# A hybrid decoder block on one core: down's weight sums built beside up instead of at the start, and a ninth pair of up by seven products

## The chip, the core and the metric

The kernel runs on one core of a Trainium2 chip. The metric is the device time of one execution in microseconds (us), and the kernel before is given by the median of three runs. The engines are named as the profile names them: PE (TensorE) multiplies matrices, DVE (VectorE) and ACT (ScalarE) do elementwise work, POOL (GpSimd) does a little elementwise work and issues some of the DMAs, SP (SyncE) issues the others. Each engine takes its own list of instructions strictly in order, and an instruction that has to wait holds up everything behind it on its engine.

## The reference

One layer of a decoder block on a sequence of 512 positions of width 1024, all in float32. The parts that matter here:

```python
mod = c_act @ ada_w[l] + ada_b[l]
shift1, scale1, gate1, shift2, scale2, gate2 = ...          # split of mod
h = rms_norm(x, norm1_g[l]) * (1 + scale1) + shift1
z = h @ w_in[l]
q, k, v, p, g_attn, g_pool = jnp.split(z, split_at, axis=-1)
...                                                         # attention of 8 heads, pooling, gates, merge
x = x + gate1 * (merged @ w_out[l])

h2 = rms_norm(x, norm2_g[l]) * (1 + scale2) + shift2
u = causal_dwconv(h2 @ w_up[l], conv_w[l], conv_b[l])       # w_up: 1024 x 5632
u_g, u_v = jnp.split(u, 2, axis=-1)
x = x + gate2 * ((jax.nn.silu(u_g) * u_v) @ w_down[l])      # w_down: 2816 x 1024
```

`ada_w` (1024 x 6144) is 25 MB, `w_up` 23 MB, `w_down` 11.5 MB.

## The kernel before

**Precision.** Every float32 operand of a product is split into a high part (`hi`, made by ACT) and the rest (`lo`, made by DVE), and a product is three matmuls, hi by hi, hi by lo and lo by hi (`mm3` and `more`, L131 to L141). A weight unit of 128 x 1024 (512 KB) is loaded by SP into one of five `wraw` buffers (`load_unit`, L82). SP's next load waits until DVE has read a buffer for the last time.

**The stages.** (1) Start: x is loaded, normalised and turned; then `p` and `q` are projected over eight channel blocks k. For each k, two units of `ada_w` (shift1 and scale1) must be loaded and summed by DVE (`sum_one`, L207) before h can be made, and for every two k there is a unit of p and one of q. (2) `k` and `v` projections. POOL takes a power of -0.5 for their norms (`hr_q`, `hr_k`, L520), DVE applies it (`n_q`, `n_k`, L528). (3) Eight heads of attention, filled up with the gate projections. (4) Branches and the output projection. (5) Up: 22 pairs j of a gate unit and a value unit. (6) Down: a Strassen-like form with seven products instead of eight, over 11 channel blocks, in seven phases.

**The weight sums.** Down's seven products need four sums of blocks of `w_down`, `t1 = b11+b12`, `t3 = b12+b22`, `t2 = t1+b22` and `t4 = b21+t2`, for eleven channel tiles kk. Ten of the tiles are made by DMAs alone (`t_step`): in six steps, a plain load fills two 256 KB buffers `ta` and `tc` (L794 is the load, L789 an accumulating DMA that adds a block of `w_down` to the buffer), and stores (L790) bring the results to HBM as `tsum`. All of these are on POOL's queue, eleven DMAs a tile, each of which waits for the one before it on its buffer. Four buffers (pool `wsum`) hold two tiles at a time. Down then loads the sums with SP (`raw_t`). Tile 4 is made by DVE instead: `t_get(4)` loads four blocks, `t_do(4)` adds them (L773 to L776), `t_put(4)` stores them.

In the code tiles 0 to 3 stand beside the heads (`t_steps(2 * h, ...)`) and tiles 5 to 10 beside the pairs of up. Only PE, DVE and ACT are issued in the order of the code (`manual_schedule`); POOL and SP are ordered by a scheduler, which puts an instruction as early as it believes that it can run. So the DMAs of tiles 0 to 3 stand at the very head of POOL's list, among the small operations of stages 1 and 2.

**Up.** A plain pair is two products of 8 blocks with 512 columns (48 matmuls). A pair in `SEVEN` (5, 7, ..., 19) is done by seven products with 256 columns (84 matmuls, `seven`), for which DVE and ACT prepare sums of the weights (`prep_seven`: steps s0 to s3, `ut`, `lo_upG`, `lo_upR`, `lo_upV`) one pair ahead; it also needs sums of h2 (`h_forms(n)`, n = 0 to 3, each two sums `hs`, two `hi` parts on ACT and two `lo` parts). Pairs 0 and 1 are multiplied ahead of the loop over j (`first`), in halves of 256 columns. At j their banks already hold the results, so the loop's first matmuls are those of pair 2. `behind(0)` is the convolution of the pair before (four DVE operations, L985 and L986) and `behind(1)` its gate (`glu_b`, two DVE operations).

**Down.** During phase 0 DVE and ACT split the weights `b11`, make the last two blocks' forms (`s_forms`) and split `s2`, which is used in phase 2.

Of the kernel before, what the change touches and what calls it, by code (L numbers as in the profile page):

```python
# [32 lines left out]
NU = (NP // 2 + 1) // 2  # L33

PLAIN = 3
SEVEN = (5, 7, 9, 11, 13, 15, 17, 19)
FORMS = ("b11", "t1", "t2", "b21", "t3", "b22", "t4")
ET = mybir.EngineType
ENG = {ET.PE, ET.DVE, ET.Activation}
# [16 lines left out]
def block_kernel(tc, x, cvec, ada, wtok, wch, pool_w, wbr, wout, wup, wdn, pack, table, out):  # L56
    nc = tc.nc
# [3 lines left out]
    with ctx:  # L61
# [692 lines left out]
        def t_tile(name):  # L754
            return tp_.tile([P, 512], F32, tag="t", name=name)

        def t_load(kk):
            i, u = divmod(kk, 2)
            b = {}
            for nm in ("b11", "b12", "b22", "b21"):  # L760
                b[nm] = t_tile(f"{nm}_{kk}")
                nc.gpsimd.dma_start(b[nm], wdn[plain[nm], i][:, u * 512 : u * 512 + 512])
            return b

        tb = {}

        def t_get(kk):
            tb[kk] = t_load(kk)

        def t_do(kk):  # L770

# [44 lines left out]
        gg = gate_stream()  # L816
        fill(gg, FIRST)
        share = (NG * 5.2 - FIRST) / H
        def t_steps(n, start, kks):

            for x_, kk in enumerate(kks):
                if 0 <= n - start - 3 * x_ < 6:
                    t_step(kk, n - start - 3 * x_)

        for h in range(H):
            pt = flip(h, rows)
            if h + 1 < H:
                rows = softmax(h + 1, *logits(h + 1))
            if h + 2 < H:
                bias_rows(h + 2)  # L830
            t_steps(2 * h, 0, range(4))
            fill(gg, 3)
            if h % 2 == 0 and h < 6:
                stacks(h // 2 + 1, False)
            elif h in (1, 3):
                stacks((h + 3) // 2, True)
            values(h, *pt)
            ada_col(2, h)
            if h == 5:
                pooling(3)  # L840
            if h == 6:
                pool_proj(3)

            t_steps(2 * h + 1, 0, range(4))
            fill(gg, 3 if h < 5 else (share - 3) / 2)
            if h < 5:
                ada_col(3, h)
            fill(gg, (share - 3) / 2)
# [89 lines left out]
        def out_norm(t):  # L938
            row = [xr[t, 0], xr[t, 1]]
            rs = rms_rows(row, f"y{t}")  # L940
            for f in range(2):
                n_ = slot(f"xn2_{t}_{f}")
                nc.vector.tensor_scalar(n_, row[f], rs, None, op0=ALU.mult)
                xn2[t, f] = n_
                x2d[t, f] = dpool.tile([P, 512], F32, name=f"x2d_{t}_{f}")
                nc.gpsimd.dma_start(x2d[t, f], row[f])

        for t in range(TT):
            for f in range(2):
                if (t, f) == (0, 0):  # L950
                    for t_ in range(2):
                        for f_ in range(2):
                            out_mm(t_, f_, 0, KT - 2)
                if (t, f) != (3, 0):
                    out_mm(t, f, KT - 2 if t < 2 else 0, KT)
                    out_post(t, f, ops[t, f])
                if late:
                    ada_col(4, late.pop(0))
                    if not late:
                        nc.vector.scalar_tensor_tensor(acol[:, 32:40], acol[:, 32:40], 1.0, pk[:, C_N2 : C_N2 + 8],  # L960
                                                       op0=ALU.add, op1=ALU.mult)
            out_norm(t)
            if t == 2:
                out_mm(3, 0, 0, KT)
                out_post(3, 0, ops[3, 0])
                flip_h2(1)
                t_get(4)

# [226 lines left out]
        for j in range(NP):  # L1197
            if j + 1 == NP:
                steps = [lambda: ahead("b11_0", 0), lambda: ahead("b11_0", 1)]
            else:  # L1200
                steps = [] if j < PLAIN else (prep_seven if j + 1 in SEVEN else prep_two)(j + 1)
            if j < 2:
                u = first[2 * j][1], first[2 * j + 1][1]
                if j == 0:
                    t_do(4)
                    t_put(4, nc.gpsimd)
                behind(0)
                if j == 1:
                    for st in prep_two(PLAIN):
                        st()  # L1210
                behind(1)
                h_forms(j)
            elif j in SEVEN:
                mine = [steps[0], lambda: behind(0), lambda: behind(1), steps[1]]
                u = seven(j, lambda n: mine[n]())
            else:
                if j < PLAIN:
                    for e in range(2):
                        upw[j, e] = ready.pop(f"up{2 * j + e}")
                u = [bank(f"u_{2 * j + e}") for e in range(2)]  # L1220
                for st in steps[:-1]:
                    st()
                up_mm(u[0], upw.pop((j, 0)), 0, S)
                behind(0)
                for st in steps[-1:]:
                    st()
                up_mm(u[1], upw.pop((j, 1)), 0, S)
                behind(1)
                if j in (2, 3):
                    h_forms(j)  # L1230
            pend.append((j, *u))
            t_steps(j, 1, range(5, 11))
            if j in ADA_AT:
                ada_col(5, ADA_AT[j])
        behind(0)
# [30 lines left out]
        def fetch(m, f):  # L1266
            for p in range(2):
                t = 2 * m + p
                x2[t, f] = slot(f"x2r_{t}_{f}")
                nc.gpsimd.dma_start(x2[t, f], x2d[t, f])  # L1270


# [4 lines left out]
        def step(acc, p, u, a, w, c0, c1, stop):  # L1277
            ac = slice(u * 256 + p * P, u * 256 + p * P + P)
            cs = slice(u * 512 + c0, u * 512 + c1)
            more(accs[acc][p][:, c0:c1], a[0][:, ac], a[1][:, ac], w[0][:, cs], w[1][:, cs],  # L1280
                 (acc, p) not in fresh, stop)
            fresh.add((acc, p))

        for n, (an, bn, acc) in enumerate(phases):
            last = n == len(phases) - 1
            held_ = []
            for i in range(NU):
                if n == 0 and i == 0:
                    ahead("b11_0", 3)
                w = unit(f"{bn}_{i}")  # L1290
                a = forms.pop((an, i))
                if last and i >= NU - 2:
                    held_.append((a, w, width(i) // 512))
                else:
                    for u in range(width(i) // 512):
                        for p in range(2):
                            step(acc, p, u, a, w, 0, 512, i == NU - 1 and u == width(i) // 512 - 1)
                if n == 0:
                    if i == 0:
                        s_forms(NU - 2)  # L1300
                    if i == 2:
                        s_forms(NU - 1)
                    split_s = fa["s2", i]
                    forms["s2", i] = split_act(split_s, f"s2_{i}", width(i) // 2)
                elif n == 1:
                    forms["a12", i] = split_act(fa["a12", i], f"a12_{i}", width(i) // 2)
                elif n == 2:
                    split_a("s3", i)
                    s2 = fa.pop(("s2", i))
                    nc.vector.tensor_add(s2, s2, fa.pop(("a12", i)))  # L1310
                    fa["s4", i] = s2
                elif n == 3:
                    split_a("s4", i)
                    split_a("a22", i)
            if last:
                for p in range(2):
                    for x_, (a, w, nu) in enumerate(held_):
                        for u in range(nu):
                            step(acc, p, u, a, w, 0, 512, x_ == len(held_) - 1 and u == nu - 1)
                    finish(p, 1, 0, "X")  # L1320
            if n == 0:
                keep("s1", "X")
            elif n == 1:
                keep("s5", "Y")
            elif n == 2:
                keep("s2", "X")
                fetch(0, 0)
            elif n == 3:
                for p in range(2):
                    finish(p, 0, 0, "Z", plus="s1")  # L1330
                fetch(1, 1)
            elif n == 4:
                for p in range(2):
                    finish(p, 1, 1, "X", minus=("s5", None))
                fetch(0, 1)
            elif n == 5:
                for p in range(2):
                    finish(p, 0, 1, "Y", minus=(None, "s2"))
                fetch(1, 0)
# [69 lines left out]
```

## Time and profile before

| | us |
|---|---|
| runs of the kernel before | 697.74, 703.54, 702.74 (median 702.74) |
| the profiled execution: its own time | 699.71 |
| the profiled execution: span from first to last instruction | 697.9 |
| PE busy in the span | 668.3 (96%) |
| DVE, ACT, POOL busy | 545.7, 367.1, 151.5 |
| matmuls | 3403 |
| moved by DMA | 139.37 MB, mean 200 GB/s |

A row of the timeline is: start and duration in us, engine, line, operation, what is written and read, how many were merged (x4), and in brackets how long the engine sat idle before it and what ended the wait. A row of the table by stretches is: from:to, length, then busy us of PE, of its weight loads, of DVE, ACT and POOL with counts, the granted clock of PE, the busy share of the DMA engines and GB/s. Matmuls overlap, so PE's rate is read from the distance between starts.

### The profile page before, as it was taken

Reading aid. Unit: us, or ns where it says so; the run is one execution under the profiler, and the core shown is the slowest. Engines: PE = TensorE matmul, PEld = TensorE weight load, DVE = VectorE, ACT = ScalarE, POOL = GpSimd, SP = SyncE. Lnnn points to the kernel's source line nnn. Section 1 sums busy time; section 2 is a strip of 40 time slices with the busy share of each in tenths; the row PEclk is TensorE's granted clock in tenths of the full one; section 3 lists DMA queues with packets and bytes.
Section 4 is the critical chain, followed back from the end, with each engine's and each line's share of the span. In section 5 each row is a group of like instructions: output and inputs, shape, how many; then the busy total and the mean of one; then the engine's idle time right before and its main releaser. Section 6 shows DMA issues by size and latency. Waiting matters only on the chain.

```text
span 697.9 us, 9445 instructions
## 1 busy us (share of the span) xinstructions
PE 668.3 (96%) x3403; PEld 567.0 (81%) x3403; DVE 545.7 (78%) x914; ACT 367.1 (53%) x631; POOL 151.5 (22%) x199
## 2 busy tenths in 40 slices
PE   7787898899999999999999999999999999999997
PEld 5565676788888888788899898889998888788886
DVE  5645697588887868887758999999898996978774
ACT  6423624466756446560364565565565563867440
POOL 5324073400000004561303434442000000001000
PEclk9989999899999999999999999999999999999999
DMA  8999769344445245769336999998334352566751
GB/s 316 336 344 338 235 170 292 113 135 136 137 162 184 96 147 122 260 216 336 142 102 199 226 289 246 309 251 245 107 121 151 76 180 81 183 229 230 291 194 60
DMA packets 44100, 139.37 MB, mean 200 GB/s; under 512 B 5795, under 2 KB 5964, under 8 KB 44054
## 3 DMA queue, kind: packets, MB, share of 16 engines
q1 hardware_dynamic: 28358, 98.23, 41.5%
q0 software_dynamic: 15696, 40.54, 22.2%
q8 instruction: 26, 0.43, 0.3%
q14 instruction: 20, 0.16, 0.1%
HBM read 123.00 MB, written 15.76 MB: 199 GB/s over the span
## 4 chain that ended last, share of the span: by engine, by line
PE 73%; DVE 5%; ACT 2%; issue 1%; POOL 0%; DMA 0%; DVEq 0%
PE u L133 7%; PE u L134 7%; PE u L135 7%; PE gate_ps L135 4%; PE gate_ps L134 4%; PE gate_ps L133 4%; PE X L141 2%; PE X L140 2%; PE X L139 2%; PE uX L141 2%; PE uX L139 2%; PE uX L140 2%; PE o L135 2%; PE o L133 2%; PE o L134 2%; PE Y L140 1%
## 5 line engine op out<-in xcount | busy, mean ns | idle before, releaser
L133 PE MATMUL u<-h2h,hi_up 128*128 128x512 f32 (+1 forms) x256 | 93.0, 363 | 0.0
L134 PE MATMUL u<-h2l,hi_up 128*128 128x512 f32 (+1 forms) x256 | 92.9, 363 | 0.0
L135 PE MATMUL u<-h2h,lo_up 128*128 128x512 f32 (+1 forms) x256 | 92.8, 362 | 0.0
L207 DVE CUSTOM_DVE_ANT_0 raw_ada<-raw_ada,cbc,pk 128x1024 f32<-128x1024 f32 x48 | 62.2, 1302 | 11.3 <-DMA raw_ada<-in_ada 9.5
L135 PEld LDWEIGHTS u<-h2h,lo_up 128*128 128x128 f32 x256 | 48.3, 189 | 7.6
L133 PEld LDWEIGHTS u<-h2h,hi_up 128*128 128x128 f32 x256 | 48.4, 189 | 7.3
L134 PEld LDWEIGHTS u<-h2l,hi_up 128*128 128x128 f32 x256 | 48.4, 189 | 7.2
L133 PE MATMUL gate_ps<-h_h,hi_gate 128*128 128x512 f32 x128 | 50.0, 390 | 0.0
L135 PE MATMUL gate_ps<-h_h,lo_gate 128*128 128x512 f32 x128 | 50.0, 390 | 0.0
L134 PE MATMUL gate_ps<-h_l,hi_gate 128*128 128x512 f32 x128 | 49.9, 390 | 0.0
L789 POOL DMA_DIRECT2D tc<-in_wdn x30 | 27.8, 928 | 26.6 <-DMA tc<-in_wdn 22.2
L124 DVE TENSOR_TENSOR lo_t<-raw_t,hi_t 128x1024 fp32r<-128x1024 f32 (+1 forms) x24 | 26.7, 1132 | 8.0 <-ACT hi_t L114 7.9
L114 ACT ACTIVATE hi_t<-raw_t 128x1024 fp32r<-128x1024 f32 (+1 forms) x24 | 23.7, 987 | 17.5 <-PE Y L141 8.4
L114 ACT ACTIVATE hi_up<-raw_up 128x1024 fp32r<-128x1024 f32 x28 | 29.2, 1050 | 4.3 <-PE u L134 4.3
L220 POOL TENSOR_TENSOR wo_l<-raw_wo,wo_h 128x512 fp32r<-128x512 f32 x16 | 25.6, 1620 | 20.3 <-ACT wo_h L219 16.5
L1083 DVE TENSOR_TENSOR lo_up<-raw_up,hi_up 128x1024 fp32r<-128x1024 f32 x22 | 26.7, 1220 | 2.9 <-ACT hi_up L114 2.9
L135 PEld LDWEIGHTS gate_ps<-h_h,lo_gate 128*128 128x128 f32 x128 | 24.0, 188 | 5.1
L133 PEld LDWEIGHTS gate_ps<-h_h,hi_gate 128*128 128x128 f32 x128 | 24.0, 188 | 4.6
L134 PEld LDWEIGHTS gate_ps<-h_l,hi_gate 128*128 128x128 f32 x128 | 24.0, 188 | 4.5
L605 ACT ACTIVATE L<-L,mn 128x512 f32<-128x512 f32 (+3 forms) x32 | 17.6, 552 | 19.2 <-DVE mn L601 19.2
L133 PE MATMUL o<-wo_h,mg_h 128*128 128x512 f32 x64 | 25.0, 391 | 0.0
L135 PE MATMUL o<-wo_h,mg_l 128*128 128x512 f32 x64 | 24.9, 389 | 0.0
(365 smaller groups left out, 2009.5 us busy)
## 6 DMA issues: line engine op xcount, KB each, us to landing
raw_ada<-in_ada SPq DMA_DIRECT2D x48, 512.0 KB, 5.4
raw_up<-in_wup SPq DMA_DIRECT2D x44, 512.0 KB, 5.5
tc<-in_wdn POOLq DMA_DIRECT2D x40, 256.0 KB, 6.6
raw_t<-tsum_t SPq DMA_DIRECT2D x20, 512.0 KB, 4.5
raw_gate<-in_wch SPq DMA_DIRECT2D x16, 512.0 KB, 4.3
ta<-in_wdn POOLq DMA_DIRECT2D x30, 256.0 KB, 6.8
raw_b<-in_wdn SPq DMA_DIRECT2D x15, 512.0 KB, 4.2
tsum_t<-ta POOLq DMA_DIRECT2D x20, 256.0 KB, 5.8
```

The lines of the kernel that those rows point to most:

```text
L114: nc.scalar.activation(hi, raw, AF.Copy)
L124: nc.vector.tensor_sub(lo, raw, hi.bitcast(F32))
L133: nc.tensor.matmul(ps, sh, mh, start=start, stop=False)
L134: nc.tensor.matmul(ps, sh, ml, start=False, stop=False)
L135: nc.tensor.matmul(ps, sl, mh, start=False, stop=stop)
L139: nc.tensor.matmul(ps, sh, mh, start=start, stop=False, skip_group_check=True)
L140: nc.tensor.matmul(ps, sh, ml, start=False, stop=False, skip_group_check=True)
L141: nc.tensor.matmul(ps, sl, mh, start=False, stop=stop, skip_group_check=True)
L207: nc.vector.tensor_tensor_reduce(out=raw, in0=raw, in1=cbc, op0=ALU.mult, op1=ALU.add, scale=1.0, scalar=col(C_AB + i), accum_out=acol[:, ...
L220: (eng or nc.vector).tensor_sub(lo[:, :w], src, hi[:, :w].bitcast(F32))
L789: add = lambda to, nm: nc.gpsimd.dma_start(to, wdn[plain[nm], i][:, us], accum_op=ALU.add)
L1083: nc.vector.tensor_sub(lo, raw, hi.bitcast(F32))
```

## The change

1. Tiles 0 to 3 are no longer made beside attention. DVE's own tile is now tile 0 instead of 4; the other ten (1 to 10) go by accumulating DMAs beside up, in the code two steps for every pair j.
2. `t_get` moves from after token block 2 to after token block 3 of the output projection. So that the scheduler can't put its loads earlier, POOL first copies a column that depends on the last norm (`rss[7]`) into each buffer.
3. Pair 3 joins `SEVEN`. For this all four `h_forms` run at j = 0 and j = 1 (before, one at each of j = 0 to 3), and `prep_seven(3)` runs at j = 2.
4. In down, the splits of `s2` stand two blocks later (the last two in phase 1), and the blocks of x that the end adds (`x2r`) use the `wsum` buffers.

```diff
-SEVEN = (5, 7, 9, 11, 13, 15, 17, 19)
+SEVEN = (3, 5, 7, 9, 11, 13, 15, 17, 19)
...
-        def t_load(kk):
+        def t_load(kk, behind_):
             i, u = divmod(kk, 2)
             b = {}
             for nm in ("b11", "b12", "b22", "b21"):
                 b[nm] = t_tile(f"{nm}_{kk}")
+                nc.gpsimd.tensor_copy(b[nm][:, :1], behind_)
                 nc.gpsimd.dma_start(b[nm], wdn[plain[nm], i][:, u * 512 : u * 512 + 512])
...
-            t_steps(2 * h, 0, range(4))
...
-            t_steps(2 * h + 1, 0, range(4))
...
             out_norm(t)
+            if t == 3:
+                t_get(0, rss[7])
             if t == 2:
...
-                t_get(4)
...
-                steps = [] if j < PLAIN else (prep_seven if j + 1 in SEVEN else prep_two)(j + 1)
+                steps = [] if j + 1 < PLAIN else (prep_seven if j + 1 in SEVEN else prep_two)(j + 1)
             if j < 2:
                 u = first[2 * j][1], first[2 * j + 1][1]
+                behind(0)
+                behind(1)
+                h_forms(2 * j, 2 * j + 1)
                 if j == 0:
-                    t_do(4)
-                    t_put(4, nc.gpsimd)
-                behind(0)
-                if j == 1:
-                    for st in prep_two(PLAIN):
-                        st()
-                behind(1)
-                h_forms(j)
+                    t_do(0)
+                    t_put(0, nc.gpsimd)
...
-                if j in (2, 3):
-                    h_forms(j)
...
-            t_steps(j, 1, range(5, 11))
+            for n in (2 * j - 2, 2 * j - 1):
+                for kk in range(1, 11):
+                    if 0 <= n - 3 * (kk - 1) < 6:
+                        t_step(kk, n - 3 * (kk - 1))
...
-                x2[t, f] = slot(f"x2r_{t}_{f}")
+                x2[t, f] = t_tile(f"x2r_{t}_{f}")
...
-                    split_s = fa["s2", i]
-                    forms["s2", i] = split_act(split_s, f"s2_{i}", width(i) // 2)
+                    if i > 1:
+                        split_s(i - 2)
                 elif n == 1:
+                    if i < 2:
+                        split_s(NU - 2 + i)
```

What this does to the order of the instructions is seen at two places. The first is the head of POOL's list, stage 1, in the kernel before (`ta`, `tc`: buffers of tiles 0 and 1; `rs_x`: the norms of x):

```order
L170 DMA pk<-in_pack 128x262
L794 DMA ta_1293<-in_wdn 128x512
L794 DMA tc_1294<-in_wdn 128x512
L794 DMA ta_1516<-in_wdn 128x512
L794 DMA tc_1517<-in_wdn 128x512
L324 TENSOR_TENSOR rs_x_172<-ms_x_170,mhalf 128x1
L324 TENSOR_TENSOR rs_x_182<-ms_x_180,mhalf 128x1
L789 DMA ta_1293<-in_wdn 128x512
```

The same place in the changed kernel:

```order
L170 DMA pk<-in_pack 128x262
L324 TENSOR_TENSOR rs_x_172<-ms_x_170,mhalf 128x1
L324 TENSOR_TENSOR rs_x_182<-ms_x_180,mhalf 128x1
L324 TENSOR_TENSOR rs_x_214<-ms_x_212,mhalf 128x1
L324 TENSOR_TENSOR rs_x_223<-ms_x_221,mhalf 128x1
L543 MEMSET kz_0_642 64x512
```

No DMA of `w_down` stands on POOL's list any more until the loads of tile 0 behind the last norm of the output projection. SP's list is the same in both kernels.

The second place is DVE's list behind the last `lo` part of the units multiplied ahead of the loop. In the changed kernel, from there to the weights of pair 3 (`b_0`: tile 0's sums; `ug`, `uv`: convolution of pair 0; `ut_3`, `lo_upG`: the first sums of pair 3's weights), less the rows that repeat:

```order
L1043 TENSOR_TENSOR hs_3566<-h2f_0_3365,h2f_2_3389 128x512
L1047 TENSOR_TENSOR hs_0_l<-hs_3566,hs_0_h 128x512
L774 TENSOR_TENSOR b_0_3286<-b_0_3286,b_0_3289 128x512
L980 SCALAR_TENSOR_TENSOR ug_3596<-u_3304,pk,ug_3596 128x511
L980 SCALAR_TENSOR_TENSOR uv_3600<-u_3335,pk,uv_3600 128x511
L1002 TENSOR_TENSOR a_0_3605<-ug_3596,uv_3600 128x256
L1043 TENSOR_TENSOR h2f_0_3365<-h2f_0_3196,h2f_0_3365 128x512
L1041 TENSOR_TENSOR h2f_0_3365<-hs_3566,h2f_2_3220 128x512
L1102 TENSOR_TENSOR ut_3_3641<-raw_up_3637,raw_up_3639 128x512
L1095 TENSOR_TENSOR lo_upG_3645<-raw_up_3637,hi_upG_3642 128x1024
```

Before, the weights of pair 3 (`lo_up`, two operations, prepared as a plain pair) stood behind `b_4`, one form of h2 and one convolution:

```order
L773 TENSOR_TENSOR b_4_3291<-b_4_3291,b_4_3293 128x512
L1048 TENSOR_TENSOR hs_3622<-h2f_0_3413,h2f_2_3437 128x512
L1052 TENSOR_TENSOR hs_0_l<-hs_3622,hs_0_h 128x512
L985 SCALAR_TENSOR_TENSOR ug_3634<-u_3352,pk,ug_3634 128x511
L985 SCALAR_TENSOR_TENSOR uv_3638<-u_3383,pk,uv_3638 128x511
L1083 TENSOR_TENSOR lo_up_3646<-raw_up_3642,hi_up_3644 128x1024
```

All sums of h2 have moved ahead of pair 3's weights on DVE, and what must be ready ahead of pair 3 is `lo_upG`, no longer `lo_up`.

More of the change, by code (lines that the diff above doesn't have):

```diff
@@ L765, in block_kernel, with t_get @@
         tb = {}
-        def t_get(kk):
-            tb[kk] = t_load(kk)
+        def t_get(kk, behind_):
+            tb[kk] = t_load(kk, behind_)
         def t_do(kk):
@@ L818, in block_kernel @@
         share = (NG * 5.2 - FIRST) / H
[L819 to L823, printed above, removed]
         for h in range(H):
@@ L940, in out_norm @@
             rs = rms_rows(row, f"y{t}")
+            rss[4 + t] = rs
             for f in range(2):
@@ L1282, in step, with split_s @@
             fresh.add((acc, p))
+        def split_s(i):
+            forms["s2", i] = split_act(fa["s2", i], f"s2_{i}", width(i) // 2)
         for n, (an, bn, acc) in enumerate(phases):
```

## The prediction, made before the changed kernel ran

> **What bounds the kernel now.** I read the page's chain of waits first, then the busy tenths, then the table by stretches and PE's waits.
>
> ```profile
> PE 73%; DVE 5%; ACT 2%; issue 1%; POOL 0%; DMA 0%; DVEq 0%
> DMA  8999769344445245769336999998334352566751
> ```
>
> The chain is PE for the most part, so the kernel is as long as PE's work plus PE's holes. The DMA digits (slices of 17.4 us) stand at 8 to 9 in the first four slices and again in slices 23 to 28, beside up. The table by stretches says what each means for PE:
>
> ```profile
> 18.00:85.20 67.20, 53.12 (x193) 40.89 (x194) 36.74 (x59) 26.01 (x43) 18.10 (x28) 0.87 1.00 321
> 119.00:126.00 7.00, 2.17 (x9) 1.67 (x8) 1.51 (x3) 0.68 (x1) 4.96 (x4) 0.68 0.75 268
> 126.00:133.00 7.00, 7.00 (x32) 5.74 (x31) 4.42 (x6) 2.43 (x3) 3.20 (x4) 0.83 0.25 75
> 400.00:500.00 100.00, 100.00 (x633) 91.06 (x632) 92.22 (x136) 60.66 (x105) 34.99 (x50) 1.00 0.92 255
> ```
>
> From 18 to 85 us (p and q) the DMA engines are full (share 1.00), every other engine has time, and PE is busy 53 of 67 us at a lowered clock (0.87). From 400 to 500 us they are nearly as full (0.92), and PE has no hole at all. So the same DMAs of the weight sums cost time in the first place and none in the second. PE's own waits name the holes:
>
> ```profile
> PE p L146 <- ACT h_h L403: 7.1, 2, 3.7
> PE T_True L550 <- DVE n_k L528: 4.8, 1, 4.8
> PE p L149 <- DVE h_l L408: 3.4, 1, 3.4
> PE X L140 <- DVE lo_b L124: 1.0, 2, 0.6
> ```
>
> The first and third lie in p and q, the second is the hole at 119 us, the fourth is in down's phase 0.
>
> **Part 1: the start without weight sums.** What follows is the loop that sets the pace of p and q, from one lo part of q to the next: SP's load of p, ACT's hi part when it has landed, DVE's lo parts; and PE's groups of four matmuls, behind a hole and undisturbed.
>
> ```profile
> 42.43 1.22 DVE L124 TENSOR_TENSOR lo_q<-raw_q,hi_q 128x1024 fp32r<-128x1024 f32 x1
> 43.68 0.33 SPq L82 DMA_DIRECT2D raw_p<-in_wtok  x1
> 53.51 1.06 ACT L114 ACTIVATE hi_p<-raw_p 128x1024 fp32r<-128x1024 f32 x1 [9.20 <-DMA raw_p<-in_wtok]
> 59.00 1.22 DVE L124 TENSOR_TENSOR lo_q<-raw_q,hi_q 128x1024 fp32r<-128x1024 f32 x1
> 40.37 2.07 PE L149 MATMUL p<-h_l,hi_p 128*128 128x512 f32 x4 [3.44 <-DVE h_l L408]
> 45.65 1.46 PE L149 MATMUL q<-lo_q,h_h 128*128 128x512 f32 x4
> 64.35 1.07 PE L149 MATMUL p<-h_h,lo_p 128*128 128x512 f32 x4
> raw_gate<-in_wch SPq DMA_DIRECT2D x16, 512.0 KB, 4.3
> raw_up<-in_wup SPq DMA_DIRECT2D x44, 512.0 KB, 5.5
> ```
>
> A turn of the loop (two blocks k) takes 59.00 - 42.43 = 16.6 us. Of it 53.51 - 43.68 = 9.8 us are the landing of p's unit, and 6.8 us the work of ACT and DVE. Undisturbed, a group of four takes 0.91 us on PE (four matmuls of 0.227 us), so a turn of 48 matmuls takes PE 10.9 us. The landing is what shrinks without the other queue: a unit of the same size lands in 4.3 us (gates, DMA half idle) or 5.5 us (up, full DMA). That bounds the turn by 11.1 and 16.6 us; I take 5.5 us for five loads in flight, so 12.3 us. Two turns gain 8.6 us.
>
> Ahead of the first turn lie 16 units (4 of x, 8 of ada, 4 of p and q), 8.4 MB. At the stretch's 321 GB/s SP alone needs 26 us for them, and with the first issue and the last sum the first lo part of a full q unit can start at 28.5 us at the earliest, not 42.43. Five buffers won't keep the queue full always: I take 31, a gain of 11.4 us (bounds 0 and 14). Together 20 us. The ceiling is PE: 192 matmuls of 0.227 us are 43.6 of the 67.2 us, so at most 23.6 us go. What is late next is PE itself, or the landing of p.
>
> Then the hole at 119 us, with DVE's last lo part ahead of it, POOL's list and the operation that PE waits for:
>
> ```profile
> 117.91 1.22 DVE L124 TENSOR_TENSOR lo_v<-raw_v,hi_v 128x1024 fp32r<-128x1024 f32 x1
> 121.03 0.57 POOL L762 DMA_DIRECT2D b<-in_wdn  x1 [3.42 <-DMA tsum_t<-tc]
> 121.61 6.47 POOL L520 TENSOR_TENSOR hr_k<-hs_k,mhalf 128x8 f32<-128x8 f32 x4
> 123.33 0.69 DVE L528 TENSOR_TENSOR n_k<-k,hr_k 128x512 f32<-128x512 f32 x1 [4.20 <-POOL hr_k L520]
> ```
>
> The four powers stood behind a DMA issue that waited for a store. Without it n_k is held only by DVE's own work and starts at 119.1: 4.2 us. PE's slow clock behind the hole (0.83 for 7 us) gives up to 1.2 us more. I take 5.5 us in all. Sum of part 1: -25.5 us.
>
> **Part 2: ten tiles beside up.** Eleven DMAs for each of ten tiles, not of six. They are on POOL's queue, where PE waits for nothing in up, and they run beside a PE without holes (400 to 500 us). I cost them at nothing; the cover is the loads' lead, five buffers for two units a pair. The tiles go in rounds of two:
>
> ```profile
> 376.49 0.54 POOL L794 DMA_DIRECT2D ta<-in_wdn  x1 [1.01 <-DMA tsum_t<-b]
> 487.94 0.58 POOL L790 DMA_DIRECT2D tsum_t<-tc  x1 [5.33 <-DMA tc<-in_wdn]
> 610.99 0.68 DVE L124 TENSOR_TENSOR lo_t<-raw_t,hi_t 128x512 fp32r<-128x512 f32 x1
> tsum_t<-tc POOLq DMA_DIRECT2D x20, 256.0 KB, 5.8
> ```
>
> With the last store's landing (5.8 us) the three rounds end at 494, 39 us a round. On this clock tile 1 will start near 390, the fifth round at 546, and its t1 is stored some 20 us later, at 566. DVE reads that sum at 611. POOL's copies ahead of tile 0's loads, the loads themselves (needed by DVE some 20 us later) and `g2`, now behind tile 10, have similar leads: nothing.
>
> **Part 3: pair 3 by seven products.** DVE's rows at the start of up, the pattern of a seven's weights at pair 5, and the starts of pair 2, pair 5 and pair 6 on PE:
>
> ```profile
> 371.78 0.69 DVE L773 TENSOR_TENSOR b<-b,b 128x512 f32<-128x512 f32 x1
> 374.57 1.28 DVE L1048 TENSOR_TENSOR hs<-h2f,h2f 128x512 f32<-128x512 f32 x2
> 377.22 0.75 DVE L985 SCALAR_TENSOR_TENSOR ug<-u,pk,ug 128x511 f32<-128x511 f32 x1
> 380.11 2.35 DVE L1083 TENSOR_TENSOR lo_up<-raw_up,hi_up 128x1024 fp32r<-128x1024 f32 x2
> 382.38 0.75 DVE L1007 TENSOR_TENSOR a<-ug,uv 128x256 f32<-128x256 f32 x2
> 401.19 0.69 DVE L1107 TENSOR_TENSOR ut<-raw_up,raw_up 128x512 f32<-128x512 f32 x1
> 401.79 1.22 DVE L1100 TENSOR_TENSOR lo_upG<-raw_up,hi_upG 128x1024 fp32r<-128x1024 f32 x1
> 409.66 1.22 DVE L1100 TENSOR_TENSOR lo_upV<-raw_up,hi_upV 128x1024 fp32r<-128x1024 f32 x1
> 375.23 0.40 PE L133 MATMUL u<-h2h,hi_up 128*128 128x512 f32 x1
> 407.90 0.28 PE L139 MATMUL uX<-h2h,hi_upG 128*128 128x256 f32 x1
> 418.13 0.23 PE u L133
> ```
>
> A plain pair takes PE (407.90 - 375.23) / 3 = 10.9 us, a seven 418.13 - 407.90 = 10.2 us. That is the whole gain: 0.7 us. Against it stands DVE's list. Between 371.78 and pair 3's first weights it now holds two forms of h2 (2.65 us each, from 374.57 to 377.22), tile 0's sums (2.8, from 371.78 to 374.57), one convolution (2.9, from 377.22 to 380.11), one gate (0.7), two more forms (5.3), `ut` (0.6) and `lo_upG` (1.2): 18.8 us, to 390.6. PE is through with pair 2 at 375.23 + 10.9 = 386.1 and waits 4.5 us. Then `lo_upV` ends 410.88 - 401.19 = 9.7 us behind the start of `ut` (a convolution stands ahead of it), so at 388.8 + 9.7 = 398.5, and three of the seven products are still to come (4.4 us): pair 3 ends at 402.9 instead of 397.0. Cost 5.9 us. The bounds are -0.7 (DVE keeps up) and +9. The rows at 40.37 and 45.65 show what follows a hole of over 3 us: four groups of four end at 47.1, so they take 6.7 us instead of 3.8; most of that would lie under the wait for `lo_upV`. I take 6.5 us. Afterwards DVE has 92 us of work per 100 and PE 100, so it doesn't fall behind again.
>
> The Trainium skill (TensorE: Matmul & The Clock Gate, Why this matters for your kernels) says that PE should not idle over about 3 us between bursts, or it falls back to half the clock. The trace agrees: the group of four behind the hole at 40.37 takes 2.07 us, not 1.07. By that rule in full pair 3 would cost some 2 us more than 5.9, by none of it nothing more.
>
> **Part 4: down.** Two splits of `s2` fewer stand ahead of the lo parts of phase 0, which cost PE 1.0 us: I take -1.0 (bounds 0 and -1). x2r in other buffers: hidden, 0.
>
> **The sum.** -25.5 + 0 + 6.5 - 1.0 = -20 us. The profiled execution took 699.7 us (span 697.9), so 679.7. It lies 1.6 us below the mean of the three runs (701.3), which I add: 681 us.
>
> **The rivals.** (a) The loads stay slow: in flight five units share their landing whoever else is on the engines, the turn stays at 16.6 us and only the shorter queue ahead of the first turn and the hole at 119 count. Then 8.6 us are missing and a little of the start: 691. For it speaks that SP's loads wait for DVE to free a buffer; against it that the share is 1.00 and that a turn moves 16.6 us x 321 GB/s = 5.3 MB, of which SP's six units are only 3.1 MB; the rest is POOL's. (b) DVE keeps up at pair 3, say since its list runs earlier than in the trace: 681 - 7.2 = 674. For it, DVE idles 4.8 us in two waits shortly ahead of 371.78:
>
> ```profile
> DVE lo_up L124 <- ACT hi_up L114: 4.8, 2, 3.1
> ```
>
> Against it, those are waits for ACT's hi parts, whose order doesn't change. (c) Slower: the weight sums come too late. The place is down's phase 1 at its last block (611 + 6 us), the price four times what a round takes over 51 us; to be slower by 1% the round must grow from 39 to 58 us, half as long again. The DMAs are then on POOL beside a DVE that is busy 92%. The trace speaks against it: at that very load three rounds took 39 us each. The Trainium skill (SBUF — State Buffer, SBUF: two separate sides) warns that DMAs issued from GpSimd starve while DVE runs a mode that takes the port shared by the two; the three rounds beside a DVE busy 92 of 100 us don't show it. (d) The start is not bound by POOL's bytes at all and only pair 3's cost is left: about 703.
>
> **How the numbers follow.** Forecast 0.62, (a) 0.13, (b) 0.15, (c) 0.05, (d) 0.05. A change below 1% (7 us) can't be told from none. Faster by over 1%: the forecast, (b) and nearly all of (a), 0.89. Within 1%: (d) and the edge of (a), 0.06. Slower: (c), 0.05. The range: 670 (p and q at PE's pace, 23.6, and half of pair 3's cost) to 692 (case (a)).
>
> **What would show it.** The stretch of p and q some 20 us shorter with a clock near 1.00 and the share of PE's wait for `h_h` down; no hole ahead of `T_True`; a new wait of PE at pair 3's `uX` for `lo_upG` and another for `lo_upV`; POOL's last store near 590 less the shift. It is wrong if turns stay at 16 us, if up has holes after pair 3, or if `raw_t` waits for a store.

## The result, and the profile after

The changed kernel takes 676.4 us (median of 6 runs, 674.95 to 677.38) against 702.1 us before (697.74 to 703.54): a ratio of 0.9645, 95% interval 0.9613 to 0.9677. The forecast was 681. The profiled execution has a span of 674.6 us, 23.3 less than before.

The busy tenths of PE and of the DMA engines, from the page after (slices of 16.9 us):

```profile
PE   8999999999999999999996999999999999999997
DMA  8976252355442476783458999999999845565661
```

PE has one slice with a hole left (the 6, slice 22), at the start of up. The table by stretches, with the columns as in the one before:

```profile
14.00:59.40 45.40, 44.76 (x195) 35.76 (x194) 36.12 (x59) 25.73 (x42) 0.00 (x0) 1.00 0.87 301
119.00:126.00 7.00, 7.00 (x37) 5.95 (x36) 6.36 (x21) 4.80 (x14) 0.00 (x0) 1.00 0.44 150
345.00:375.00 30.00, 23.83 (x128) 21.36 (x127) 27.80 (x44) 16.56 (x27) 15.07 (x22) 0.83 0.81 211
400.00:500.00 100.00, 100.00 (x637) 91.29 (x636) 90.99 (x136) 59.15 (x101) 42.60 (x60) 1.00 0.99 271
```

p and q now fill the 45.4 us from 14 to 59.4 with a PE at full clock. Beside up the DMA share went from 0.92 to 0.99, and PE is as full as it was. At pair 3 (345 to 375) PE is busy 23.8 of 30 us at a clock of 0.83, while DVE is busy 27.8. PE's own waits, after (engine, tile and line that waits, what it waits for, then us in total, times, longest us):

```profile
PE uX L139 <- ACT hi_upG L1090: 3.5, 1, 3.5
...
PE uX L141 <- DVE lo_upG L1095: 1.4, 1, 1.4
PE uX L139 <- ACT ka L1143: 1.2, 1, 1.2
PE B L133 <- ACT hi_br L114: 0.6, 1, 0.6
PE p L146 <- ACT h_h L403: 0.6, 2, 0.3
...
PE T_True L550 <- DVE n_k L528: 0.5, 1, 0.5
```

The old waits for `h_h`, `h_l` and `n_k` have shrunk from 15.3 to 1.1 us; the three at pair 3's `uX` are new. `X L140`, down's wait, has gone.

**Where the 23.3 us come from.** PE's first matmul of up cuts the kernel in two. The row of `u` on PE shows its time (the first after "us,"), in the kernel before and after:

```profile
L133 PE MATMUL u<-h2h,hi_up x256: 277/389/396, 350.5 to 585.9; 128*128 128x512 f32 x96, 128*128 128x256 f32 x32
```

```profile
L133 PE MATMUL u<-h2h,hi_up x240: 278/390/397, 318.7 to 563.8; 128*128 128x512 f32 x88, 128*128 128x256 f32 x32
```

Up starts 31.8 us earlier (forecast 25.5). From there to the end the kernel before takes 697.9 - 350.5 = 347.4 us and the changed one 674.6 - 318.7 = 355.9 us: 8.5 us more (forecast 5.5: 6.5 for pair 3 less 1.0 for down). 31.8 - 8.5 = 23.3. This cut is used for every kernel below, because it holds to some 0.3 us between kernels that don't differ behind it, while whole runs of the kernel before spread over 6 to 8 us.

### The profile page after: what moved, and what is told of

It reads as the page before. It is cut to its first block, busy times and chain, and to the rows that moved or that the text cites. A ratio compares the mean times of both kernels' runs of the same rounds, so it can differ in the third digit from the quotient of the medians.

```text
span 674.6 us, 9543 instructions
## 1 busy us (share of the span) xinstructions
PE 659.8 (98%) x3439; PEld 564.4 (84%) x3439; DVE 549.7 (81%) x923; ACT 370.7 (55%) x641; POOL 153.3 (23%) x203
## 5 line engine op out<-in xcount | busy, mean ns | idle before, releaser
L133 PE MATMUL u<-h2h,hi_up 128*128 128x512 f32 (+1 forms) x240 | 86.9, 362 | 0.0
L134 PE MATMUL u<-h2l,hi_up 128*128 128x512 f32 (+1 forms) x240 | 86.8, 362 | 0.0
L135 PE MATMUL u<-h2h,lo_up 128*128 128x512 f32 (+1 forms) x240 | 86.7, 361 | 0.0
L135 PEld LDWEIGHTS u<-h2h,lo_up 128*128 128x128 f32 x240 | 45.4, 189 | 6.8
L133 PEld LDWEIGHTS u<-h2h,hi_up 128*128 128x128 f32 x240 | 45.4, 189 | 6.6
L134 PEld LDWEIGHTS u<-h2l,hi_up 128*128 128x128 f32 x240 | 45.4, 189 | 6.5
L114 ACT ACTIVATE hi_up<-raw_up 128x1024 fp32r<-128x1024 f32 x26 | 27.2, 1050 | 4.3 <-PE u L134 4.3
L1078 DVE TENSOR_TENSOR lo_up<-raw_up,hi_up 128x1024 fp32r<-128x1024 f32 x20 | 24.3, 1220 | 4.3 <-ACT hi_up L114 4.3
```

The lines of the kernel that those rows point to most:

```text
L114: nc.scalar.activation(hi, raw, AF.Copy)
L133: nc.tensor.matmul(ps, sh, mh, start=start, stop=False)
L134: nc.tensor.matmul(ps, sh, ml, start=False, stop=False)
L135: nc.tensor.matmul(ps, sl, mh, start=False, stop=stop)
L1078: nc.vector.tensor_sub(lo, raw, hi.bitcast(F32))
```

## The experiments

All of them in one table; the medians of before were 701.0 to 701.7 us in these comparisons.

| kernel | us, median | ratio to before, 95% | up's first matmul | from there to the end |
|---|---|---|---|---|
| before | 701 to 702 | 1 | 350.5 | 347.4 |
| after | 676.4 | 0.961 to 0.968 | 318.7 | 355.9 |
| sums_only | 668.0 | 0.949 to 0.957 | 317.8 | 347.5 |
| plain3 | 666.4 | 0.947 to 0.954 | 318.0 | 346.2 |
| pair3_only | 710.1 | 1.007 to 1.016 | 348.7 | 355.7 |
| reorder | 674.6 | 0.959 to 0.966 | 318.7 | 354.3 |
| reorder2 | 669.3 | 0.949 to 0.958 | 318.7 | 348.9 |
| warm | 675.4 | 0.959 to 0.968 | 318.4 | 355.1 |
| tiny | 668.5 | 0.949 to 0.957 | 318.7 | 347.4 |
| tiny_up | 675.0 | 0.959 to 0.966 | 318.3 | 356.1 |
| dup | 703.2 | 1.000 to 1.005 | 346.5 | 356.1 |
| dup_plain | 693.1 | 0.982 to 0.994 | 335.0 | 356.1 |

### The parts alone

**sums_only**: the kernel before with the weight sums moved as in the change, and nothing else.

```
-            t_steps(2 * h, 0, range(4))
...
-                t_get(4)
+            if t == 3:
+                t_get(0, rss[7])
...
-            t_steps(j, 1, range(5, 11))
+            for n in (2 * j - 2, 2 * j - 1):
+                for kk in range(1, 11):
+                    if 0 <= n - 3 * (kk - 1) < 6:
+                        t_step(kk, n - 3 * (kk - 1))
```

> The kernel before with the weight sums alone moved (tile 0 loaded late, tiles 1 to 10 in accumulating DMAs beside up, none beside attention); pair 3 stays plain and down stays as it was. Theory (the gain is the start's, the other two edits are separate prices): PE reaches pair 2 some 31.8 us earlier, as in the changed kernel, and up has no hole, so 702.1 - 31.8 = 670. Rival (the ten tiles beside up cost something that pair 3's wait covers in the changed kernel): a hole of PE in up, 672 to 676. My forecast's own figure for this part was 25.5 us: 676.6.

668.0 us, below what either theory gave. Up starts at 317.8, and from there to the end it takes 347.5 us, as before (347.4). So the whole of the start's gain, 32.7 us, is this part's, and ten tiles beside up instead of six cost nothing that can be measured.

**plain3**: the changed kernel with pair 3 plain.

```
-SEVEN = (3, 5, 7, 9, 11, 13, 15, 17, 19)
+SEVEN = (5, 7, 9, 11, 13, 15, 17, 19)
...
-                steps = [] if j + 1 < PLAIN else ...
+                steps = [] if j < PLAIN else ...
...
+                behind(0)
+                if j == 1:
+                    for st in prep_two(PLAIN):
+                        st()
+                behind(1)
+                h_forms(j)
...
+                if j in (2, 3):
+                    h_forms(j)
```

> The changed kernel with pair 3 plain again and the forms of h2 where the kernel before has them; weight sums and down as changed. Theory (pair 3 by seven costs 9.8 us: pair 2 starts 31.8 us earlier than before but pair 4 only 22.0): 676.4 - 9.8 = 666.6. Rival (DVE is behind at up's start whatever pair 3 is, so the wait moves to pair 5's weights): at most 2 us of gain, 674 or more. By the forecast's figure of 6.5 us: 670.

666.4 us, as the theory had it (666.6): the wait does not move to pair 5. From up's start to the end 346.2 against 355.9: pair 3 by seven products costs 9.7 us. Against sums_only (347.5) it is 1.3 us shorter: that is down's edit. This kernel beats both, by some 10 us and 35 us.

**pair3_only**: the kernel before with pair 3 by seven and the forms moved.

```
-SEVEN = (5, 7, 9, 11, 13, 15, 17, 19)
+SEVEN = (3, 5, 7, 9, 11, 13, 15, 17, 19)
...
+                behind(0)
+                behind(1)
+                h_forms(2 * j, 2 * j + 1)
```

> The kernel before with pair 3 by seven products and the forms of h2 moved as in the change; the weight sums and down stay. Theory (the cost is DVE's list ahead of pair 3 and has nothing to do with the sums beside up): the same 9.8 us, 702.1 + 9.8 = 712, with PE waiting for hi_upG, lo_upG and ka. Rival (the tile DMAs beside it, at a DMA share of 0.81 instead of 0.78, delay pair 3's weights): less than 5 us, below 707. By the forecast's figure of 6.5 us: 708.6.

710.1 us, and 355.7 against 347.4 from up's start to the end: 8.3 us, with the same three waits (3.4, 1.3 and 1.2 us) though only the old tiles run beside it. The rival, tile DMAs that delay pair 3's weights, falls. That the cost is 8.3 and not 9.7 us is PE's clock: behind the last of the three waits pair 3 takes 403.44 - 396.14 = 7.3 us here and 8.6 in the changed kernel (366.26 to 374.86, shown below), where the first of its matmuls takes 0.58 us and not 0.39. Why the clock came back earlier here stays open.

```profile
396.14 0.39 PE L139 MATMUL uX<-hs_h,hi_upR 128*128 128x256 f32 x1 [1.23 <-ACT ka L1148]
...
403.44 0.40 PE L133 MATMUL u<-h2h,hi_up 128*128 128x512 f32 x1
```

The median of 710.1 includes a start that varies by some 2 us: in the profiled execution, 706.2 us, up begins at 348.7, not 350.5.

### What pair 3 waits for

This is the changed kernel's trace there: DVE's rows from pair 0's `ug` on, and ACT's around `ka`.

```profile
348.35 0.74 DVE L980 SCALAR_TENSOR_TENSOR ug<-u,pk,ug 128x511 f32<-128x511 f32 x1
...
358.09 0.68 DVE L1102 TENSOR_TENSOR ut<-raw_up,raw_up 128x512 f32<-128x512 f32 x1
358.69 1.22 DVE L1095 TENSOR_TENSOR lo_upG<-raw_up,hi_upG 128x1024 fp32r<-128x1024 f32 x1
...
364.46 0.75 DVE L981 SCALAR_TENSOR_TENSOR ug<-u,pk,ug 128x510 f32<-128x510 f32 x1
```

```profile
357.36 1.13 ACT L1090 ACTIVATE hi_upG<-raw_up 128x512 fp32r<-128x512 f32 x2
...
365.30 0.63 ACT L995 ACTIVATE ug<-ug 128x512 f32<-128x512 f32 x1 [0.42 <-DVE ug L981]
365.84 0.36 ACT L1143 ACTIVATE ka<-uX 128x256 f32<-128x256 f32 x1
```

And PE's rows:

```profile
354.14 0.39 PE L135 MATMUL u<-h2h,lo_up 128*128 128x512 f32 x1
358.02 0.39 PE L139 MATMUL uX<-h2h,hi_upG 128*128 128x256 f32 x1 [3.50 <-ACT hi_upG L1090]
...
359.96 0.58 PE L141 MATMUL uX<-h2h,lo_upG 128*128 128x256 f32 x1 [1.44 <-DVE lo_upG L1095]
...
366.26 0.58 PE L139 MATMUL uX<-hs_h,hi_upR 128*128 128x256 f32 x1 [1.23 <-ACT ka L1143]
...
374.86 0.40 PE L133 MATMUL u<-h2h,hi_up 128*128 128x512 f32 x1
```

Pair 3 ends with the start of pair 4 at 374.86, 20.5 us behind the end of pair 2. ACT comes to `hi_upG` at 357.36, behind hi parts of the forms that wait for DVE, and DVE to `ut` at 358.09 and to `lo_upG` right behind it, so PE waits 3.5 + 1.4 = 4.9 us for G's weights. The third product adds to accumulator X, which ACT must first copy out (`ka`); `ka` stands in ACT's list behind the silu of pair 1, and this waits for DVE's convolution (`ug`, 364.46). Once the accumulator is copied, five products follow without a wait, and nothing is waited for at `lo_upV`.

**reorder**: the changed kernel, pair 3's weights ahead of the last two forms, tile 0's adds later.

```
-                h_forms(2 * j, 2 * j + 1)
                 if j == 0:
-                    t_do(0)
-                    t_put(0, nc.gpsimd)
+                    h_forms(0, 1)
...
+                early_ = steps if j == 2 else steps[:-1]
+                for st in early_:
                     st()
                 up_mm(u[0], upw.pop((j, 0)), 0, S)
+                if j == 2:
+                    h_forms(2, 3)
                 behind(0)
...
+                if j == 2:
+                    t_do(0)
+                    t_put(0, nc.gpsimd)
```

> The changed kernel with DVE's list at the start of up in another order and nothing else: the forms hs2 and hs3 behind pair 3's weights, tile 0's four adds and stores at the end of pair 2 instead of in pair 0, pair 3's V weights ahead of pair 1's convolution. Theory (what PE waits for at pair 3 is DVE's list): lo_upG ends some 8 us earlier (two forms 5.3 and the adds 2.8 fewer ahead of it), before PE is through with pair 2, and pair 3 costs 0 to 3 us instead of 9.8: 667 to 670. Rival (the loads of pair 3's units or ACT's hi parts arrive no earlier): the waits stay, 674 to 677.

Half a miss. Its waits (the first row of PE's waits):

```profile
PE uX L139 <- ACT ka L1143: 7.2, 1, 7.2
```

The waits for `hi_upG` and `lo_upG` are gone, so DVE's list did set them, and the loads did not. But the time is 674.6, in the rival's range, for another reason: the wait for `ka`, 1.2 us in the changed kernel, is now 7.2. DVE's list ahead of the silu got shorter only by tile 0's adds (2.8) less `lo_upV` (1.2), so `ka` comes 1.6 us earlier than before, and from up's start to the end the gain is just that: 354.3 against 355.9. The first wait had been covering the second.

**reorder2**: in addition `ka` gets out of the silu's way, the last two forms move into pair 3, and tile 0's adds go from DVE to POOL.

```
+                if j == 3:
+                    mine = [lambda: h_forms(2, 3), lambda: (steps[0](), behind(0)),
+                            lambda: (behind(1), behind(0)), lambda: (steps[1](), behind(1))]
...
-            nc.vector.tensor_add(b["b11"], b["b11"], b["b12"])
+            nc.gpsimd.tensor_add(b["b11"], b["b11"], b["b12"])
```

(the other three adds of tile 0 likewise; in pair 2 neither convolution nor gate.)

> The changed kernel with the lists of DVE and ACT at the start of up in a third order: pair 3's weights first, the forms hs2 and hs3 inside pair 3 behind its first product, the convolutions and silu of pairs 1 and 2 behind ACT's copies ka, and tile 0's four adds on POOL. In the last order tried the wait for lo_upG was gone, but PE waited 7.2 us for ka, which stood behind a silu that waited for DVE. Theory (ka's place in ACT's list is the second bound): that wait shrinks to 1 us or less and pair 3 costs 0 to 3 us instead of 8: 666 to 670. Rival (DVE has more work there than PE in any order): the wait comes back at pair 4's or pair 5's weights, 672 to 675.

669.3 us, inside the theory's range. PE's waits at pair 3:

```profile
PE uX L139 <- ACT kb L1143: 1.8, 1, 1.8
...
PE uX L139 <- ACT ka L1143: 0.5, 1, 0.5
```

The wait for `ka` fell from 7.2 to 0.5 us, and pair 3 costs 348.9 - 346.2 = 2.7 us more than plain. So both lists, DVE's and ACT's, are shown as the cause; what each of the three moves gained by itself is not shown. What is left is mostly `kb`, in ACT's list. The rival (the wait comes back at pair 4 or 5) is not seen beyond a 0.3 us wait for `lo_up`. Even so seven products don't pay here.

**warm**: the changed kernel with 74 matmuls of no use in the holes.

```
+            def warm(n):
+                for _ in range(n if j == 3 else 0):
+                    nc.tensor.matmul(Zb[:, 256:], h2h[0][:, :P], h2h[1][:, 256:], start=True, stop=True)
+
+            warm(40)
             prod("a11", "b11", X, True)
...
+            warm(34)
             prod("s2", "t2", X, False)
```

> The changed kernel with PE kept busy in pair 3's holes by matmuls whose results nobody reads (into an unused half of a PSUM bank): 40 of 128x256 ahead of the first product (40 x 0.12 = 4.8 us for the holes of 3.5 and 1.4) and 34 ahead of the third (4.1 us). In the changed kernel's trace some 40 matmuls behind the first hole follow each other at 0.213 us and not 0.120. Theory (the slow clock lies mostly under the wait for ka, which ACT has ready at 366.2 whatever PE does): the clock stays at 1.00, the third product starts at the same time, and only its five products at full speed gain 1 to 2 us: 675. Rival (the clock is what costs beside the holes themselves, some 4 us): 672.

675.4 us. The rows of PE with the fillers:

```profile
354.09 4.96 PE L1148 MATMUL uZ<-h2h,h2h 128*128 128x256 f32 x40
...
362.43 4.24 PE L1148 MATMUL uZ<-h2h,h2h 128*128 128x256 f32 x34
366.51 0.28 PE L139 MATMUL uX<-hs_h,hi_upR 128*128 128x256 f32 x1
```

```profile
365.57 0.36 ACT L1144 ACTIVATE ka<-uX 128x256 f32<-128x256 f32 x1
```

The clock stays up (one matmul 0.28 us, not 0.58 and 0.41). From the third product on pair 3 takes 373.71 - 366.51 = 7.2 us (pair 4 starts at 373.71) instead of 374.86 - 366.26 = 8.6, so of the 9.7 us the slow clock there is 1.4 us. What it slowed ahead of that lay under the wait for `ka`, which ACT has ready 47.5 us behind up's start in both kernels. Only 0.8 us are gained from up's start to the end, because the second group of fillers ends at 366.51 and itself holds up the third product by some 0.5 us.

The Trainium skill (TensorE: Matmul & The Clock Gate, Why this matters for your kernels) says that an idle of over about 3 us takes PE back to half the clock; the changed kernel's trace agrees (behind the hole of 3.5 us some 40 matmuls follow at 0.213 us each, not 0.120). A shorter hole did it too: in the kernel before, four matmuls behind a hole of 1.75 us take 28.39 - 26.51 = 1.9 us, not 0.91, so 3 us are no safe limit here.

```profile
26.51 2.08 PE L146 MATMUL p<-h_h,p0h 128*128 128x512 f32 x4 [1.75 <-ACT h_h L401]
28.39 1.55 PE L149 MATMUL p<-h_h,p0l 128*128 128x512 f32 x4
```

### What was slow at the start

**tiny**: the kernel before with the early tiles' DMAs cut to 8 columns.

```
-            us = slice(u * 512, u * 512 + 512)
+            us = slice(u * 512, u * 512 + (8 if kk < 4 else 512))
```

> The kernel before; the DMAs of tiles 0 to 3 stay where they are in POOL's list, in number, order and waits, but each moves 8 of its 512 columns (those four tiles' sums are thus left out but for 8 columns, and down loads plain blocks of the same size in their place). Theory (bytes on the DMA engines are what slows p and q): p and q run as in the changed kernel, in about 46 us from 14, and the issue ahead of hr_k waits for a short store, so 702 - 32 = 670, or up to 676 if the hole at 119 us stays. Rival (the number of DMAs, their issue on POOL and their waits in its queue are what costs, whatever they carry): 695 or more.

668.5 us: up starts at 318.7, exactly where the changed kernel has it, with POOL's DMAs in the same number and order. The rival falls: it is what the DMAs carry. Yet the table by stretches, first of the kernel before and then of tiny, has

```profile
14.00:59.40 45.40, 34.66 (x131) 26.72 (x131) 26.67 (x47) 16.19 (x28) 15.80 (x24) 0.84 1.06 338
```

```profile
14.00:59.40 45.40, 44.11 (x192) 34.92 (x191) 36.41 (x59) 25.65 (x41) 26.29 (x39) 1.00 0.99 306
```

a DMA share of 0.99, beside a PE that is busy 44.1 of 45.4 us, where the kernel before has 1.06 and a PE busy 34.7 us (the view's share can pass 1). A full share by itself doesn't say that loads are late.

**dup**: the changed kernel with the four tiles' DMAs back beside attention.

```
+        def agains(n):
+            for kk in range(4):
+                if 0 <= n - 3 * kk < 6:
+                    again(kk, n - 3 * kk)
...
+            agains(2 * h)
             fill(gg, 3)
...
+            agains(2 * h + 1)
```

(`again` is the old `t_step` with stores into spare tensors.)

> The changed kernel with the four tiles' eleven DMAs each put back beside attention, at the places in POOL's list that the kernel before has for them, into tensors that nobody reads; the ten tiles beside up stay. Theory (what was gained at the start is lost by them alone): the start is the old one, 676.4 + 32 = 708, with lo parts of q every 16 us and the hole ahead of n_k. Rival (part of the gain came from something else, such as the order in which the loads of x, ada and p are issued): 690 to 700.

703.2 us, 5 below the theory and 3 above the rival's range. The loop is the old one: lo parts of q at 41.99, 58.75 and 74.86 us, and up starts 27.8 us later than in the changed kernel. What is missing is the hole ahead of `n_k`: PE waits 1.0 us there, not 4.8. In the kernel before the four powers of k stood behind tile 4's load `b`, which waited for a store; dup has no such load there, and its `T_True` starts 4.2 us earlier than before, at 119.95 and not at 124.17. So the four tiles cost 27.8 us and the rest of the 31.8, 4.0 us, is put down to tile 4's load; as up's start varies by some 2 us between kernels with the old start (350.5 and 348.7), these two are no more exact than that.

```profile
119.95 0.63 PE L550 MATMUL T_True<-pk,n_q 128*128 128x128 f32 x4 [1.01 <-DVE n_k L528]
```

**dup_plain**: the same with plain loads for the accumulating ones.

```
-            add = lambda to, nm: nc.gpsimd.dma_start(to, src(nm), accum_op=ALU.add)
+            add = lambda to, nm: nc.gpsimd.dma_start(to, src(nm))
```

> The last kernel but with plain loads in place of the accumulating ones: the changed kernel plus the four tiles' DMAs beside attention, same number, places, sizes and stores, into tensors that nobody reads. Theory (any bytes of a second queue take the place of p's and q's): the same as with accumulating loads, 703, lo parts of q some 16 us apart and p's unit landing in 9 us. Rival (accumulating is what makes these DMAs dear, since they also read what they add to): p's unit lands in 5 to 7 us and the time is 685 to 697.

693.1 us: the rival's range, though the unit of p lands no faster at first (40.57 to 49.05, 8.5 us; then 55.80 to 61.86, 6.1 us). Up starts at 335.0, so plain loads of the same bytes cost 335.0 - 318.7 = 16.3 of the 27.8 us; that they accumulate costs the other 11.5, to within the 2 us by which up's start varies. So the theory's bytes are the larger part and the rival's accumulating is the rest. The same stretch in the kernel before, in dup and in dup_plain:

```profile
18.00:59.40 41.40, 30.77 (x104) 23.02 (x105) 23.82 (x41) 14.72 (x25) 14.01 (x22) 0.84 1.06 341
```

```profile
18.00:59.40 41.40, 29.51 (x114) 22.60 (x113) 24.61 (x42) 15.38 (x27) 13.86 (x21) 0.87 1.06 336
```

```profile
18.00:59.40 41.40, 32.41 (x122) 24.47 (x121) 27.29 (x44) 15.70 (x27) 14.36 (x27) 0.92 1.01 391
```

The engines are full in all three (1.06, 1.06 and 1.01), but move 391 GB/s with plain loads and 336 to 341 with accumulating ones. The Trainium skill (Collectives: The Full Stack, The bandwidth ceiling: the fold count and why AG ≠ RS ≠ AR) says of ReduceScatter that its add needs two source reads where a copy needs one. An accumulating load is no collective; the lower rate here points the same way, but no run here counted the reads.

**tiny_up**: the changed kernel with the tiles beside up cut to 8 columns.

```
-            us = slice(u * 512, u * 512 + 512)
+            us = slice(u * 512, u * 512 + 8)
```

> The changed kernel with 8 of 512 columns in each DMA of tiles 1 to 10 beside up (those sums are left out but for 8 columns, and down loads plain blocks of the same size in their place). Theory (ten tiles beside up cost PE nothing, and pair 3's waits are DVE's and ACT's lists): no change, 675 to 678, the waits at pair 3 as they were. Rival (a DMA share of 0.81 to 0.99 delays the units of pair 3 or DVE): 670 or less.

675.0 us, 356.1 from up's start to the end (355.9 with the full tiles), the waits for pair 3's weights as they were (3.5 and 1.4); PE waits 2.1 us for `ka`, not 1.2, and the third product starts at the same 47.6 us behind up's start. Beside up the ten tiles are free.

## Why the prediction was right, and where it wasn't

The direction and the mechanism held. The total of 681 missed 676.4 by 4.6 us: part 1 gained 6.3 us more than forecast, pair 3 and down together gave back 3.0 more, and the 1.6 us added for the median over the profiled run were not there in the kernel after (its profiled run lies at the median). That the first two misses offset each other is luck. The range's lower end does not follow from its own terms: p and q at PE's pace (3.6 us more) and half of pair 3's cost (3.2) take 681 to 674, not to 670; the measured time lies above both.

**p and q (20 us; measured 25.7).** These are the rows after that answer to the loop's: lo_q on DVE, then SP's load of p and ACT's hi part.

```profile
28.60 1.21 DVE L124 TENSOR_TENSOR lo_q<-raw_q,hi_q 128x1024 fp32r<-128x1024 f32 x1
39.74 1.22 DVE L124 TENSOR_TENSOR lo_q<-raw_q,hi_q 128x1024 fp32r<-128x1024 f32 x1
51.17 1.21 DVE L124 TENSOR_TENSOR lo_q<-raw_q,hi_q 128x1024 fp32r<-128x1024 f32 x1
```

```profile
29.84 0.33 SPq L82 DMA_DIRECT2D raw_p<-in_wtok  x1
```

```profile
34.24 1.06 ACT L114 ACTIVATE hi_p<-raw_p 128x1024 fp32r<-128x1024 f32 x1 [3.77 <-DMA raw_p<-in_wtok]
```

Both sums went to their best ends. The first lo part came at 28.6 us; 28.5 was named as the earliest, and 31 was taken. A turn is 11.1 and 11.4 us, with p's unit landing in 34.24 - 29.84 = 4.4 us; 12.3 was taken from up's median landing of 5.5, where the gates' 4.3 would have been the nearer row: at p and q the DMA engines are no longer full (0.87). That makes 13.8 + 10.2 us where 11.4 + 8.6 were forecast. Behind the last lo part PE gained 1.7 us more by its clock (in the kernel before, the groups of four at 73.52 and 75.01 take 1.5 and 1.7 us, behind a hole of 3.45 us). The step that failed is the ceiling, "at most 23.6 us go": it counted PE's work only from 18 us on. PE's first matmul of p moved too:

```profile
18.02 1.20 PE L146 MATMUL p<-h_h,p0h 128*128 128x512 f32 x4
```

```profile
13.99 1.17 PE L146 MATMUL p<-h_h,p0h 128*128 128x512 f32 x4
```

These 4.0 us, of the loads ahead of p, lie outside the stretch that the ceiling was taken from.

**That it is POOL's bytes.** Right, by tiny (up starts where the changed kernel has it); rivals (a) and (d) fall with it. (The 703 of (d) was itself too low: with only pair 3's cost and down's gain left, 701.3 + 6.5 - 1.0 is 707.) But the argument was short: 5.3 MB a turn, of which 3.1 are SP's, treated a byte as a byte, and in dup_plain the same bytes cost 16.3 us, not 27.8.

**The hole at 119 us (5.5).** Measured: `T_True` starts at 94.17 instead of 124.17, 30.0 earlier, of which 25.7 are from p and q; so 4.3, and 1.8 more up to up's start: 6.1. Some 1.2 of the 1.8 are the clock behind the hole (0.83 for 7 us before, 1.00 after); the rest is not traced. Right, and dup, without the load `b` ahead of the powers, has 1.0 us of the wait left. The rows before and after:

```profile
124.17 1.09 PE L550 MATMUL T_True<-pk,n_q 128*128 128x128 f32 x4 [4.83 <-DVE n_k L528]
```

```profile
94.17 0.63 PE L550 MATMUL T_True<-pk,n_q 128*128 128x128 f32 x4 [0.53 <-DVE n_k L528]
```

**Ten tiles beside up (0).** Right: 347.5 against 347.4 in sums_only. A round was given as 39 us; POOL's first load of tile 1 and its last store show it.

```profile
349.26 0.54 POOL L795 DMA_DIRECT2D ta<-in_wdn  x1
...
540.78 0.56 POOL L791 DMA_DIRECT2D tsum_t<-tc  x1 [4.21 <-DMA tc<-in_wdn]
```

Five rounds in 191.5 us and a landing of some 5: 39.4 us each. Only the end was wrong (590 less the shift, so some 565; it is 541): some 15 us because tile 1 starts at 349 and not near 390 less the shift, the rest because five rounds of 39 us from 390, less the landing, put the last store at 579 and not at 590. Rival (c) was the further off for it.

**Pair 3 (6.5 us; measured 9.7).** Of its two waits the first was right in cause and size: 4.5 us forecast for `lo_upG`, 4.9 measured, 3.5 of them at ACT's `hi_upG`, which DVE's list holds up as well. The second was named wrongly. The step that failed is "Then `lo_upV` ends ..., and three of the seven products are still to come": ACT's list was not followed there, and `ka`, two products earlier, holds PE until 366.26, with five products behind it. Up to there pair 3 is 9.0 us late (366.26, less the end of pair 2 at 354.14 + 0.23, less two products of 24 matmuls of 0.12, 2.9); the slow clock behind it adds 1.4, where 0.6 was taken (6.5 for 5.9), and the gain of 0.7 goes off: 9.7. reorder and reorder2 show the place of `ka`: with the weights early PE waits for it 7.2 us, with `ka` early too it is 0.5. Rival (b) falls.

**Down (-1.0).** Right, if a little outside its bounds of 0 and -1: -1.3 by plain3 against sums_only, and the wait `X L140` is gone.

The part that would have been dropped with this knowledge is pair 3: without it the kernel takes 666.4 us.

## What to carry to other kernels

Before a background transfer is called free, look for a stage where PE has no hole at a nearly full DMA share, and put it there: the same sums cost 28 us beside p and q and nothing beside up. A step that saves PE 0.7 us is worth nothing where DVE already works almost without a pause (27.8 of 30 us) and ACT waits for it: count what they must do first, and follow the in-order list of each engine to the instruction that frees PE's accumulator, not only to the one that makes its weights. When one wait is taken away, the next in line may have been hidden by it almost whole.

## What was not expected of the hardware

Accumulating DMAs took up the DMA engines longer than plain loads of the same bytes: 336 GB/s against 391 in the same stretch at a full share, and of the 27.8 us that the four tiles cost, some 11.5 are due to it. And DMAs of 8 columns hold the share at 0.99 while a 512 KB load beside them lands nearly as fast as without them (issued at 30.28 us in tiny, ACT's hi part at 35.13: 4.8 us, against 4.4 in the changed kernel and 9.8 before). So a full share doesn't tell engines that hold up a load from engines that hardly do; the landing time of the load that is waited for does.
